# Reordering roundings and subtractions in a two-layer fp32 trunk on one core

## The chip, the cores and the metric

The kernel runs on one core of a Trainium2 chip. The metric is device time in microseconds (us), the median of several runs. TensorE (PE) multiplies; VectorE (DVE) and ScalarE (ACT) work elementwise; GpSimd (POOL) and SyncE (SP) issue loads here. Each engine takes its instructions from a queue of its own, and they meet at semaphores.

## The reference

Two layers, each with a feed-forward block, a mixer and a second feed-forward block, on x of 512 tokens by 1024 channels in float32:

```
x += 0.5 * swiglu_1(rmsnorm(x))
h  = rmsnorm(x);  z = h @ w_in        # pool input, q, k, v, two gate logits
x += (g_pool * P_pool(pool_mixer) + g_attn * P_attn(window_attention)) @ w_out
x += 0.5 * swiglu_2(rmsnorm(x))
swiglu(h): g, u = split(h @ w_gu);  (silu(g) * u) @ w_down      # inner width 2816
```

## The kernel before

**Three products for one.** Every large product is made of three float32r matmuls. Each operand is a pair: a high part (ScalarE rounds the float32 value to float32r by a copy) and a low part (VectorE subtracts the high part from the value, so it must wait for the copy). The terms are high x high, high x low of the weight, low x high of the activation. In the trace `wh` and `wl` are the parts of the weights, `xgh`/`xgl` and `more` those of the activations in the feed-forward block, `op` those in its down product.

**Seven products for eight.** The feed-forward products use a Strassen-like scheme of seven products, in the order `a11, s1, s2, a12, s3, s4, a22`. Its operands are quarters of the activation and combinations of them: B11, T1, T2, B21, T3, B22, T4 in this order for the first product (the gate and up product, a "block"), and in the down product `a11`, f["a"], ... made from the turned results. Combinations of the weights (`sums`) are added on VectorE. A product is run in four segments (c, q), c a half of the contraction with its own weight tile, q a row half; a segment is six matmuls (three in the second half of a 384 column down product). A half product is the two segments of one c. `mid[kind, c, q]` names work that is issued after a segment; `steps[kind]` evacuates the product.

**The inner width** is worked in groups of two blocks and one down product: 384, 512 and 512 columns in ffn0, and 512, 384, 512 in the others. ffn0 and ffn1 are the first and second feed-forward block of layer 0, ffn2 and ffn3 those of layer 1; between ffn0 and ffn1, and between ffn2 and ffn3, stands a mixer. So there are twelve down products, three to a feed-forward block. The last of each is `final`: it also feeds the next norm.

**The norm.** The scale 1/rms is applied after the product, so what is fed is x times the gain. `feed(q, i, pt)` turns a quarter of x (channel pairs q, token half i) with four PE transposes into a PSUM bank, scales it on ScalarE into `xg` (or `more`, when it is kept), and rounds it with `halve`. For a feed-forward block (`halves`) `t1`, `t3`, `t2`, `t4` then combine the kept quarters on VectorE; j counts two tiles of each. T3 has its combination (`t3`) and its rounding (`t3_split`) apart.

**halve and split.** Both round on ScalarE. `split` subtracts at once. `halve` puts the subtraction on the list `unsettled`, and `settle()` issues what stands there:

```
def halve(hi, lo, src):
    nc.scalar.copy(out=hi, in_=src)
    unsettled.append(lambda: nc.vector.tensor_tensor(out=lo, ...))
```

`settle()` runs before each piece of `mid` work and after each product's step, so that a subtraction stands in VectorE's queue behind what was issued meanwhile.

**The order** is written out by hand; the engines keep program order. `W.prep()` after each half product issues, ahead of use, the low part of the weight tile three half products on, the sums, the high part four on, and the loads into seven raw buffers, as they come free (by SP, with the second summand added in by POOL). What a final down product leaves undone for the next block is put on the list `pend` by `left(nxt)`: for a feed-forward block `t3` twice, `t2` twice, two feeds, `t3_split` twice, `t4` twice; for the mixer two feeds. Each call of `due()` takes the next. PSUM holds three tiles of two banks for products (`roles`) and one for turning (`turn`); feeds use a bank of `roles[2]` and one of `turn` by turns.

**The down product** (`down`). The combination `t4` (in the trace `fa<-fa,pt`) reads the turning bank. `high(name, ...)` rounds an operand on ScalarE, `low(name)` subtracts. The updates of x (`x<-mm,x`) stand in the steps of a11, s1, s2, a12, s3, s4, a22; in a final one each quarter of x that is done is squared on ScalarE (`sq`) for the next norm, or stored in the last block.

**The mixer's start.** Two PSUM tiles `late` take the first two pool tiles: `begun(0)` multiplies K tiles 0 to 3 of tile 0, then of tile 1; `begun(1)`, after a part of the q, k, v product, K tiles 4 to 7. K tiles 0 and 1 come from feeds q=0, 2 and 3 from feeds q=1, which are the last feeds of the down product in front.

Of the kernel before, what the change touches and what calls it, by code (L numbers as in the profile page):

```python
# [22 lines left out]
KT = D // P  # L23
# [3 lines left out]
B11, T1, T2, T3, T4, B21, B22 = range(7)  # L27
# [81 lines left out]
def trunk(ctx, tc, x0, xT, consts, vecs, rows, w_g4, w_g3, w_d8, w_d6, w_qkv, w_u, w_pool, w_gate, w_br, w_out, out):  # L109
# [204 lines left out]
    def term(pt, i, n, wh, wl, ah, al):  # L314
        nc.tensor.matmul(pt, wh, ah, start=i == 0, stop=False)
        nc.tensor.matmul(pt, wh, al, start=False, stop=False)
        nc.tensor.matmul(pt, wl, ah, start=False, stop=i == n - 1)
# [30 lines left out]
    class Norm:  # L348
# [61 lines left out]
        def t1(self, j):  # L410
            d = temp("d")
            nc.vector.tensor_tensor(out=d, in0=self.keep[0, j], in1=self.keep[1, j], op=ALU.subtract)
            split(*self.both(T1, j), d)

        def t3(self, j):
            self.keep[4, j] = t = self.place(1, 2, j, F32)
# [2 lines left out]
        def t2(self, j):  # L419
            t = self.keep[0, j]  # L420
            nc.vector.scalar_tensor_tensor(
                out=t, in0=t, scalar=-1.0, in1=self.keep[4, j], op0=ALU.mult, op1=ALU.subtract
            )
            split(*self.both(T2, j), t)

        def t3_split(self, j):
            split(*self.both(T3, j), self.keep[4, j])

        def t4(self, j):
            u = temp("t4")  # L430
            nc.vector.scalar_tensor_tensor(
                out=u, in0=self.keep[0, j], scalar=-1.0, in1=self.keep[3, j], op0=ALU.mult, op1=ALU.subtract
            )
            split(*self.both(T4, j), u)

        def first(self, j, src, scale):
            d = temp("d")[:, :HT]
# [80 lines left out]
    def due(bank=None):  # L518
        if pend:
            pend.pop(0)(bank)  # L520
# [9 lines left out]
    def ffn(ctx, nm, nxt, last):  # L530
# [129 lines left out]
        def low(name):  # L660
            ops.pop((name, "low"))()
# [103 lines left out]
        def down(n, final):  # L765

            jn = n // P

            def add(t, d, c):
                def go(pt):  # L770
                    y = x[:, 2 * t:2 * t + 2, d * S:(d + 1) * S]
                    nc.vector.scalar_tensor_tensor(out=y, in0=pt, scalar=c, in1=y, op0=ALU.mult, op1=ALU.add)
                return go

            def whole(t, d, qs=range(2)):
                if not final:
                    return
                for q in qs:
                    b = 2 * t + q
                    if last:  # L780
                        nc.sync.dma_start(
                            out=out[b * P:(b + 1) * P, d * S:(d + 1) * S], in_=x[:, b, d * S:(d + 1) * S]
                        )
                    else:
                        nxt.squares(d, b)

            def a11(pt):
                add(0, 0, 0.5)(pt)
                return flush

            def s1(pt):
                add(1, 1, -0.5)(pt)
                nc.vector.tensor_tensor(out=f["b"], in0=f["c"], in1=f["b"], op=ALU.subtract)

            def s2(pt):
                add(1, 0, 0.5)(pt)
                low("s3")

            def a12(pt):
                add(0, 0, 0.5)(pt)  # L800
                ops.pop("t4")()
                whole(0, 0)

            def s3(pt):
                add(1, 1, -0.5)(pt)
                low("a22")
                whole(1, 1)

            def s4(pt):
                add(1, 0, 0.5)(pt)  # L810
                whole(1, 0)
                if final:
                    W.sums = None

            def a22(pt):
                y = x[:, 0:2, S:2 * S]
                for q in range(2):
                    nc.vector.scalar_tensor_tensor(
                        out=y[:, q, :], in0=pt[:, q, :], scalar=-0.5, in1=y[:, q, :], op0=ALU.mult, op1=ALU.add
                    )  # L820
                    whole(0, 1, [q])

            mid = {
                ("a11", 1, 0): lambda: low("s2"), ("s1", 0, 1): lambda: low("a12"),
                ("s2", 0, 1): lambda: high("s3", f["b"], n), ("a12", 0, 1): lambda: high("s4", f["c"], n),
                ("s3", 0, 0): lambda: low("s4"), ("s3", 0, 1): lambda: high("a22", f["a"], n),
            }
            if final and nxt is not None:
                spot = [t[:, 0, :] for t in (roles[2], turn)]
                feed = lambda q, t, at: lambda: nxt.feed(q, t, spot[at])  # L830
                mid.update({
                    ("s3", 1, 0): feed(0, 0, 0), ("s3", 1, 1): feed(1, 0, 1), ("s4", 0, 1): feed(2, 1, 0),
                    ("s4", 1, 1): feed(3, 1, 1), ("a22", 0, 1): feed(0, 1, 0), ("a22", 1, 0): feed(1, 1, 1),
                })
                if nxt.halves:
                    mid["a22", 1, 1] = lambda: [nxt.t1(j) for j in range(2)]
                left(nxt)

            strassen(
                ORDER, S, (2, jn - 2), lambda kind, k, q: [ops[kind][:, i, q, k * P:(k + 1) * P] for i in range(2)],  # L840
                dict(a11=a11, s1=s1, s2=s2, a12=a12, s3=s3, s4=s4, a22=a22), mid,
            )

# [5 lines left out]
        for gi, (_, group) in enumerate(groups(nm is first)):  # L849
            for i, n in enumerate(group):  # L850
                if nm is first and gi == i == 0:
                    plain(n, xt, acc, later)
                else:
                    mid = {}
                    if nm is first:
                        if gi == 0:
                            mid["s1", 1, 1] = flush
                    elif gi == i == 0:
                        mid = {at: due for at in (
                            ("a11", 0, 0), ("a11", 0, 1), ("s1", 0, 0), ("s1", 0, 1), ("a12", 0, 0), ("a12", 0, 1),  # L860
                            ("s3", 0, 1), ("s3", 1, 1),
                        )}
                        mid["s1", 1, 1] = lambda: due(turn[:, 0, :])
                        mid["s2", 0, 1] = lambda: due(roles[2][:, 0, :])
                    block(n, i, ORDER, mid)
            down(n, gi == 2)

    @with_exitstack
    def mix(ctx, l, nm, nxt):
# [225 lines left out]
        late = [mm() for _ in range(2)]  # L1095
        w = [W.take("u") for _ in range(2)]

        def begun(h):
            for i in range(2):
                for k, t in enumerate(nm.terms(w[i])[4 * h:4 * h + 4]):  # L1100
                    term(late[i], 4 * h + k, KT, *t)
                if h:
                    W.prep()

        begun(0)
        settle()
        due(side_bank[0])
        for q, width in ((False, 256), (True, 512)):
            pts = [t[:, :width] for t in (mm(), mm(), wide[:, 0, :], wide[:, 1, :])]
            per = CH // width  # L1110
            for c in range(KT // per):
                w_ = W.take("qkv")
                for b in range(NB):
                    for k in range(per):
                        kt, cols = per * c + k, slice(k * width, (k + 1) * width)
                        rows = slice(b % 2 * P, (b % 2 + 1) * P)
                        term(
                            pts[b], kt, KT, *(t[:, kt // 2, b // 2, kt % 2, rows] for t in (nm.h, nm.l)),
                            w_[0][:, cols], w_[1][:, cols],
                        )  # L1120
                    if not q and c == 0 and b == 1:
                        settle()
                        due(side_bank[1])
                    if not q and c == 1 and b == 1:
                        nm.spread(side_bank[1])
                        for i in range(2):
                            pooled(i, late[i])
                if not q and c == 0:
                    settle()
                    nm.sums()  # L1130
                    praw = temp("praw")
                    nc.sync.dma_start(out=praw, in_=w_pool[l])
                    begun(1)
                if c + 1 < KT // per:
                    W.prep()
                if q and c == 1:
                    side(-2)
            for b in range(NB):
                nc.scalar.activation(
                    out=(qs[b] if q else kv[:, b]).rearrange("p h d -> p (h d)"),  # L1140
                    in_=pts[b], func=AF.Copy, scale=nm.rstd[:, b:b + 1],
                )
            W.prep()
            if not q:
                split(*spare[4], praw)
            side(-1 if q else -3)
# [196 lines left out]
```

## Time and profile before

| | |
|---|---|
| median of 3 runs | 1888.84 us (1888.61 to 1888.88) |
| the profiled execution | 1888.9 us, of which the span from the first to the last instruction is 1887.0 us |
| granted TensorE clock | 0.999 |
| busy: PE, VectorE, ScalarE, GpSimd | 98%, 77%, 53%, 7% |
| DMA | 292.80 MB, mean 155 GB/s |

How to read the rows: a row of the timeline is start, length, engine, line, operation, output<-inputs, shape, and in brackets how long the engine stood idle before and who ended that. All instructions have line 97, that of the helper which records them, so rows are told apart by their tiles: `mm`, `sc`, `pt`, `pt_tp`, `pt_pv` are PSUM tiles, `x` is the residual, `cst,x` marks a transpose. A row of the table of waits is engine, output, who ended the wait, us in total, times, longest. A row of the windows is the stretch, its length, and the busy time (count) of PE, weight loads, VectorE, ScalarE and GpSimd, then PE clock, DMA share and GB/s. Starts and lengths are in us.

### The profile page before, as it was taken

The numbers are of one execution on the slowest core, as the hardware profiler recorded it, in microseconds if no ns is written. First come the engines' busy times: TensorE is split into PE (matmuls) and PEld (weight loads), VectorE is DVE, ScalarE is ACT, GpSimd is POOL, SyncE is SP. The second block draws the span as 40 slices with busy tenths as digits, with TensorE's granted clock in tenths as the row PEclk, the third lists the DMA queues.
The fourth block names the chain that finished last, engine by engine and source line by source line (L and its number), as shares of the span: only waits on it lengthen the run. The fifth ranks groups of instructions, "written<-read, shape, count | busy, mean of one in ns | idle before, by whom it ended". The sixth has DMA issues, their size and how long they took to land.

```text
span 1887.0 us, 23912 instructions
## 1 busy us (share of the span) xinstructions
PE 1858.3 (98%) x8928; PEld 1555.4 (82%) x8928; DVE 1448.5 (77%) x1829; ACT 1008.6 (53%) x1493; POOL 124.5 (7%) x152
## 2 busy tenths in 40 slices
PE   9999999999999999999999999999999999999998
PEld 8888888887788788988878898888877887899887
DVE  7878878677564988887988878786675648888878
ACT  6555455645454654555665555555554446545553
POOL 0100000000000001110001001100000000001000
PEclk9999999999999999999999999999999999999999
DMA  8687666322223676777657667753212237667763
GB/s 251 179 229 180 193 174 171 125 80 77 79 89 101 166 199 161 183 204 188 170 158 196 157 179 206 191 166 107 90 68 90 93 86 203 171 168 184 218 179 100
DMA packets 87571, 292.80 MB, mean 155 GB/s; under 512 B 9856, under 2 KB 10112, under 8 KB 87456
## 3 DMA queue, kind: packets, MB, share of 16 engines
q1 hardware_dynamic: 67104, 223.47, 35.1%
q0 software_dynamic: 20208, 67.78, 20.4%
q8 instruction: 70, 1.15, 0.2%
q14 instruction: 45, 0.37, 0.1%
q10 hardware_dynamic: 144, 0.03, 0.0%
HBM read 289.15 MB, written 2.10 MB: 154 GB/s over the span
## 4 chain that ended last, share of the span: by engine, by line
PE 80%; DVE 12%; ACT 6%; issue 1%; DMA 1%; SPq 0%; DVEq 0%; ACTq 0%
PE mm L97 73%; DVE wl L97 4%; PE sc L97 4%; DVE sums L97 2%; PE pt L97 2%; ACT wh L97 2%; PE pt_pv L97 1%; DVE x L97 1%; DVE more L97 1%; ACT xgh L97 1%; DVE op L97 1%; ACT xg L97 1%; PE pt_tp L97 1%; DVE fa L97 1%; ACT sq L97 1%
## 5 line engine op out<-in xcount | busy, mean ns | idle before, releaser
L97 ACT CAST wh<-raw 128x1024 fp32r<-128x1024 f32 (+3 forms) x443 | 432.9, 988 | 274.9 <-PE mm L97 197.0
L97 DVE TENSOR_TENSOR wl<-raw,wh 128x1024 fp32r<-128x1024 f32 (+3 forms) x443 | 502.2, 1146 | 90.5 <-PE mm L97 57.8
L97 PE MATMUL mm<-wh,op 128*128 128x512 f32 x1232 | 392.1, 394 | 2.4 <-DVE op L97 2.4
L97 PE MATMUL mm<-wh,more 128*128 128x512 f32 (+1 forms) x1104 | 335.2, 374 | 3.8 <-ACT more L97 2.6
L97 PE MATMUL mm<-wl,xgh 128*128 128x512 f32 (+2 forms) x840 | 310.4, 370 | 5.9 <-DVE wl L97 5.6
L97 PE MATMUL mm<-wh,xgh 128*128 128x512 f32 (+2 forms) x840 | 312.2, 372 | 1.3 <-ACT xg L97 0.8
L97 PE MATMUL mm<-wh,xgl 128*128 128x512 f32 (+2 forms) x840 | 309.8, 369 | 0.9 <-DVE xgl L97 0.9
L97 PEld LDWEIGHTS mm<-wh,op 128*128 128x128 f32 x1232 | 230.6, 188 | 52.4 <-DVE op L97 5.8
L97 PE MATMUL mm<-wl,op 128*128 128x512 f32 x616 | 240.3, 390 | 1.6 <-DVE wl L97 1.6
L97 PEld LDWEIGHTS mm<-wh,more 128*128 128x128 f32 x1104 | 204.7, 188 | 36.8 <-ACT more L97 3.3
L97 PE MATMUL mm<-wl,more 128*128 128x512 f32 (+1 forms) x552 | 206.6, 374 | 1.7 <-DVE wl L97 1.7
L97 DVE TENSOR_TENSOR wl<-sums,wh 128x1024 fp32r<-128x1024 f32 (+1 forms) x140 | 159.0, 1137 | 45.0 <-ACT wh L97 28.7
L97 ACT CAST wh<-sums 128x1024 fp32r<-128x1024 f32 (+1 forms) x140 | 136.2, 981 | 95.0 <-DVE sums L97 52.2
L97 PEld LDWEIGHTS mm<-wl,xgh 128*128 128x128 f32 x840 | 157.9, 188 | 31.1 <-DVE wl L97 10.3
L97 PEld LDWEIGHTS mm<-wh,xgh 128*128 128x128 f32 x840 | 157.8, 188 | 23.5 <-ACT xg L97 2.1
L97 PEld LDWEIGHTS mm<-wh,xgl 128*128 128x128 f32 x840 | 157.8, 188 | 23.2 <-DVE xgl L97 2.1
L97 POOL DMA_DIRECT2D raw<-in_w_g x92 | 79.5, 864 | 1325.5 <-DMA raw<-in_w_g 591.6
L97 PEld LDWEIGHTS mm<-wl,op 128*128 128x128 f32 x616 | 115.8, 188 | 26.2 <-DVE wl L97 3.3
L97 PE MATMUL mm<-xgh,wh 128*128 128x512 f32 x320 | 129.4, 404 | 0.4 <-ACT xgh L97 0.4
L97 PE MATMUL mm<-xgl,wh 128*128 128x512 f32 x320 | 125.3, 392 | 0.4 <-DVE xgl L97 0.4
L97 PE MATMUL mm<-xgh,wl 128*128 128x512 f32 x320 | 125.2, 391 | 0.0
L97 PEld LDWEIGHTS mm<-wl,more 128*128 128x128 f32 x552 | 103.6, 188 | 18.5 <-DVE wl L97 3.3
(247 smaller groups left out, 2397.7 us busy)
## 6 DMA issues: line engine op xcount, KB each, us to landing
raw<-in_w_g SPq DMA_DIRECT2D x160, 512.0 KB, 5.0
raw<-in_w_d SPq DMA_DIRECT2D x100, 512.0 KB, 4.5
raw<-in_w_g POOLq DMA_DIRECT2D x64, 512.0 KB, 6.9
raw<-in_w_g SPq DMA_DIRECT2D x77, 384.0 KB, 4.3
raw<-in_w_d POOLq DMA_DIRECT2D x40, 512.0 KB, 5.5
raw<-in_w_gate SPq DMA_DIRECT2D x32, 512.0 KB, 3.2
raw<-in_w_g POOLq DMA_DIRECT2D x28, 384.0 KB, 5.8
raw<-in_w_br SPq DMA_DIRECT2D x16, 512.0 KB, 3.2
```

What stands on the lines that cost most here:

```text
L97: return lambda *args, **kw: self.tc.keep_in_program_order(call(*args, **kw))
```

## The change

Five edits.

1. `t1`, `t2`, `t3_split` and `t4` of the norm use `halve` instead of `split`: the rounding is issued at once, the subtraction at the next `settle()`.
2. In every down product `t4` moves from the step of a12 to behind the first segment of s3, and the low part of s4 from there into the step of a12; the high part of a22 moves from the second to the third segment of s3, its low part from the step of s3 to behind the first segment of s4.
3. In final down products that feed a norm, the first feed moves from the third to the second segment of s3, and the third feed from the second to the third segment of s4.
4. In the first block after a mixer or down product (not in ffn0) the first `t2` comes behind the third segment of a11 and the second behind the first of s1 (they were behind the first and second of s1), and the two feeds behind the third segment of s1 and the first of s2 (they were behind the fourth of s1 and the second of s2).
5. The mixer's first two tiles take K tiles 0 and 1 of both tiles, then 2 and 3 of both.

```diff
@@ Norm
         def t1(self, j):
-            split(*self.both(T1, j), d)
+            halve(*self.both(T1, j), d)
...
-            split(*self.both(T2, j), t)
+            halve(*self.both(T2, j), t)
...
-            split(*self.both(T3, j), self.keep[4, j])
+            halve(*self.both(T3, j), self.keep[4, j])
...
-            split(*self.both(T4, j), u)
+            halve(*self.both(T4, j), u)
@@ down
             def a12(pt):
                 add(0, 0, 0.5)(pt)
-                ops.pop("t4")()
+                low("s4")
                 whole(0, 0)
             def s3(pt):
                 add(1, 1, -0.5)(pt)
-                low("a22")
                 whole(1, 1)
...
-                ("s3", 0, 0): lambda: low("s4"), ("s3", 0, 1): lambda: high("a22", f["a"], n),
+                ("s3", 0, 0): lambda: ops.pop("t4")(), ("s3", 1, 0): lambda: high("a22", f["a"], n),
+                ("s4", 0, 0): lambda: low("a22"),
...
-                    ("s3", 1, 0): feed(0, 0, 0), ("s3", 1, 1): feed(1, 0, 1), ("s4", 0, 1): feed(2, 1, 0),
+                    ("s3", 0, 1): feed(0, 0, 0), ("s3", 1, 1): feed(1, 0, 1), ("s4", 1, 0): feed(2, 1, 0),
@@ ffn
-                            ("a11", 0, 0), ("a11", 0, 1), ("s1", 0, 0), ("s1", 0, 1), ("a12", 0, 0), ("a12", 0, 1),
+                            ("a11", 0, 0), ("a11", 0, 1), ("a11", 1, 0), ("s1", 0, 0), ("a12", 0, 0), ("a12", 0, 1),
                             ("s3", 0, 1), ("s3", 1, 1),
...
-                        mid["s1", 1, 1] = lambda: due(turn[:, 0, :])
-                        mid["s2", 0, 1] = lambda: due(roles[2][:, 0, :])
+                        mid["s1", 1, 0] = lambda: due(turn[:, 0, :])
+                        mid["s2", 0, 0] = lambda: due(roles[2][:, 0, :])
@@ mix
-        def begun(h):
+        def begun(ks):
             for i in range(2):
-                for k, t in enumerate(nm.terms(w[i])[4 * h:4 * h + 4]):
-                    term(late[i], 4 * h + k, KT, *t)
-                if h:
+                terms = nm.terms(w[i])
+                for k in ks:
+                    term(late[i], k, KT, *terms[k])
+                if ks[-1] == KT - 1:
                     W.prep()
-        begun(0)
+        begun((0, 1))
+        begun((2, 3))
...
-                    begun(1)
+                    begun((4, 5, 6, 7))
```

## Prediction

> **What bounds the kernel now.** I read the page's busy times first, then the table of waits, then two stretches by windows, then the timeline around each stretch the diff touches.
>
> ```profile
> PE 1858.3 (98%) x8928; PEld 1555.4 (82%) x8928; DVE 1448.5 (77%) x1829; ACT 1008.6 (53%) x1493; POOL 124.5 (7%) x152
> PE mm L97 <- DVE op L97: 2.4, 9, 0.4
> 606.00:656.00 50.00, 46.75 (x206) 36.13 (x205) 41.66 (x58) 33.40 (x48) 3.45 (x4) 1.00 0.51 137
> 656.00:690.00 34.00, 34.00 (x155) 28.24 (x154) 25.79 (x24) 17.51 (x21) 2.59 (x3) 1.00 0.77 215
> ```
>
> PE is the bound nearly everywhere: 34.00 us busy of the 34.00 from 656 on. So only PE's waits can be won. The change alters no instruction's size and no engine's count, only the order on VectorE, ScalarE and PE. From 606 to 656 (ffn1's first block) PE idles 3.25 us and VectorE works 41.66 of 50.
>
> Idle time understates a wait, because a matmul's bar overlaps the next. These rows of an ordinary 512 column down show it:
>
> ```profile
> 213.56 0.62 PE L97 MATMUL mm<-wh,op 128*128 128x512 f32 x2
> 214.01 0.39 PE L97 MATMUL mm<-wl,op 128*128 128x512 f32 x1
> 214.59 0.73 PE L97 MATMUL mm<-wh,op 128*128 128x512 f32 x2 [0.19 <-DVE op L97]
> 622.14 0.50 PE L97 MATMUL mm<-wh,more 128*128 128x512 f32 x1 [0.70 <-ACT more L97]
> 622.48 0.40 PE L97 MATMUL mm<-wl,more 128*128 128x512 f32 x1
> ```
>
> Two matmuls start in 214.01 - 213.56 = 0.45, so one start takes 0.227. The next start comes after 0.58: 0.35 lost, where the bar tells of 0.19. After a wait the following start also takes longer (622.14 to 622.48, 0.34): 0.11 more. So I price waits from starts: 0.35 + 0.11 = 0.46 here. [...]
>
> **The downs.** There are 12: five of 512 columns without feeds, four of 384, three final ones with feeds.
>
> ```profile
> 209.92 1.22 DVE L97 SCALAR_TENSOR_TENSOR x<-mm,x 128x1024 f32<-128x1024 f32 x1
> 211.06 1.21 DVE L97 SCALAR_TENSOR_TENSOR fa<-fa,pt 128x1024 f32<-128x1024 f32 x1
> 212.18 1.22 DVE L97 TENSOR_TENSOR wl<-sums,wh 128x1024 fp32r<-128x1024 f32 x1
> 213.32 1.22 DVE L97 TENSOR_TENSOR op<-fc,op 128x1024 fp32r<-128x1024 f32 x1
> 816.57 0.50 PE L97 MATMUL mm<-wl,op 128*128 128x512 f32 x1 [0.42 <-DVE wl L97]
> 817.44 0.73 PE L97 MATMUL mm<-wh,op 128*128 128x512 f32 x2 [0.37 <-DVE op L97]
> 819.04 0.95 DVE L97 TENSOR_TENSOR op<-fa,op 128x768 fp32r<-128x768 f32 x1
> ```
>
> VectorE runs x, t4 (`fa`), weight low, then s4's own low; 1024 columns take 1.135 from start to start. The change swaps t4 and s4's low: the low then ends at 212.3, before PE asks at 214.24, and the weight low stays where it was. Gain 0.46. t4 ends at 214.5, a22's high copy at 215.6, a22's low third behind the x update at 219.1; its product starts at 219.2 and reads it at 219.7. Covered. Five times 0.46 = 2.3.
>
> In a 384 down s4 waits twice: for the weight low (816.57), unchanged, then for the low: 817.44 - 816.57 - 0.227 = 0.64, which goes. But a22's low (819.04) now runs behind the weight low of its product: they change places, so it starts at 819.04 + 1.135 and ends at 821.12. PE, 0.64 early, asks at 821.0: a new wait of 0.17 + 0.11. Gain 0.36, four times 1.4. With no restart cost it is 1.9; with a full VectorE instruction more in front (1.135) a loss of 3.1.
>
> **Final downs into the mixer (ffn0, ffn2).**
>
> ```profile
> 337.14 0.52 PE L97 MATMUL mm<-cst,x 128*128 128x128 f32 x3 [1.07 <-ACT xgh L97]
> 341.57 1.22 DVE L97 SCALAR_TENSOR_TENSOR x<-mm,x 128x1024 f32<-128x1024 f32 x1
> 342.99 0.63 ACT L97 ACTIVATE sq<-x 128x512 f32<-128x512 f32 x1
> 346.68 0.69 DVE L97 TENSOR_TENSOR xgl<-xg,xgh 128x512 fp32r<-128x512 f32 x1 [0.17 <-ACT xgh L97]
> 347.47 0.46 PE L97 MATMUL mm<-xgl,wh 128*128 128x512 f32 x1
> 349.03 0.51 PE L97 MATMUL mm<-xgh,wh 128*128 128x512 f32 x1 [0.18 <-ACT xgh L97]
> 349.76 0.50 PE L97 MATMUL mm<-xgl,wh 128*128 128x512 f32 x1 [0.22 <-DVE xgl L97]
> 353.74 0.27 PE L97 MATMUL pt_tp<-cst,x 128*128 128x128 f32 x1
> ```
>
> The feed at 337.14 waits 1.2 for s3's x update (1.07 idle and 0.39 - 0.227 of the last bar). One segment later (six matmuls, 1.36) it need not wait. But PE does not keep the 1.2. t4, now one instruction pair later, ends at 333.0 and holds the turning bank for the second feed (0.3 lost); s4's x update stands behind lows of the feeds, at 341.7, so the feed in a22 waits 0.6 for it; and ScalarE's squares of it start at 343.0 as before, so the mixer's first low is ready at 347.37 as before. PE's second mixer matmul starts at 347.42 instead of 347.47: 0.05 won, bounds 0 and 0.6.
>
> There the new K order pays. Second K pair starts before: 349.03 and 349.76; from 347.47 to the transpose at 353.74 are 6.27 for 23 starts, 5.22 without waits. Twelve matmuls of both tiles' first K pair now come first, so PE asks for the second pair at 350.0, after the lows (349.7). Gain 6.27 - 5.22 - 0.11 = 0.94. Together 1.0, twice 2.0.
>
> **First blocks (ffn1, ffn3).** Here T1 to T4 are rounded and subtracted.
>
> ```profile
>   ACT more L97: 3.2, 4
> 616.14 1.22 DVE L97 TENSOR_TENSOR wl<-raw,wh 128x1024 fp32r<-128x1024 f32 x1
> 620.75 0.69 DVE L97 SCALAR_TENSOR_TENSOR more<-more 128x512 f32<-128x512 f32 x1
> 622.12 0.69 DVE L97 TENSOR_TENSOR more<-more 128x512 fp32r<-128x512 f32 x1 [0.69 <-ACT more L97]
> 626.44 0.69 DVE L97 TENSOR_TENSOR xgl<-xg,xgh 128x512 fp32r<-128x512 f32 x1 [0.51 <-ACT xgh L97]
> 634.98 1.29 DVE L97 TENSOR_TENSOR more<-more 128x512 fp32r<-128x512 f32 x2
> 638.45 1.22 DVE L97 TENSOR_TENSOR r<-r,mm 128x1024 f32<-128x1024 f32 x1
> 642.53 0.69 DVE L97 TENSOR_TENSOR more<-t,more 128x512 fp32r<-128x512 f32 x1 [1.13 <-ACT more L97]
> 615.70 1.00 ACT L97 COPY r<-mm 128x1024 f32<-128x1024 f32 x1
> 640.81 0.39 PE L97 MATMUL mm<-wh,xgh 128*128 128x512 f32 x1
> 644.41 0.50 PE L97 MATMUL mm<-wl,xgh 128*128 128x512 f32 x1 [0.49 <-DVE wl L97]
> 647.62 0.47 PE L97 MATMUL mm<-wh,more 128*128 128x512 f32 x1 [0.41 <-ACT wh L97]
> 648.66 0.50 PE L97 MATMUL mm<-wl,more 128*128 128x512 f32 x1 [0.57 <-DVE wl L97]
> 654.01 1.03 PE L97 MATMUL pt<-cst,p 128*128 128x128 f32 x8
> ```
>
> The first row is from the view of the `more` tiles in this block: VectorE sat idle 3.2 us, in front of four subtractions, until ScalarE had rounded. I walked the three queues instruction by instruction with these durations (on VectorE 1.135 and 0.605 from start to start); in the old order the walk meets every row above within 0.1. In the new order:
> - VectorE: T2's first combination directly behind the weight low of 616.14, at 617.3 instead of 620.75; two sums 617.9 and 619.0; weight low 620.5; T2's first low 621.65; second combination 622.3; weight low 622.9; second low 624.0. The first rounding stands on ScalarE ahead of r's copy (now 618.5, was 615.70) and of s2's weight highs (0.9 later). s2 still starts at 621.1, 1.0 earlier; it then waits 0.6 for the weight low and T2's low, and half the gain stays.
> - T2's two stalls go, but the B21 low then waits for ScalarE (T2's rounding, a weight high, two scalings, its own rounding: 623.0 to 626.0) until 626.0, was 626.44. VectorE is 0.44 ahead, and so up to T3's first low (634.5).
> - T3's second low is settled only after r's add. Behind the first one stand a weight low (635.1), a sum (636.3) and r (637.4, was 638.45); it starts at 638.55 instead of 635.6. PE asks at 638.1 and waits until 639.28. So s4 starts at 641.65, 0.84 later than 640.81. This is the price of the deferral.
> - T4's two stalls go, so the weight lows of s4 and a22 come in time. The waits of 644.41, 647.62 and 648.66 (0.65, 0.58, 0.82, and 0.11 twice) go: 2.3.
> - The block ends at 652.53 instead of 654.01: 1.5 won, twice 3.0.
>
> [...] If VectorE could pass r's add, T3's waits would go and the time would be 1873.8.
>
> **Final down into ffn2.**
>
> ```profile
> 948.31 0.69 DVE L97 TENSOR_TENSOR xgl<-d,xgh 128x512 fp32r<-128x512 f32 x1 [1.09 <-ACT xgh L97]
> 992.40 1.03 PE L97 MATMUL pt<-cst,p 128*128 128x128 f32 x8
> ```
>
> T1 is made here on a full VectorE, and its stalls (1.09 at the first) delay s1's weight low. Settled behind x's last update, the two subtractions find their rounding done, and the weight low comes 1.26 earlier. The same walk, with PE 0.66 early from the down, meets the same T3 wait (1.2) and ends the block at 989.5: 2.9 won.
>
> **Sum.** 2.3 + 1.4 + 2.0 + 3.0 + 2.9 = 11.6. The profiled execution took 1888.9 (span 1887.0), 0.06 over the median 1888.84. Forecast 1888.9 - 11.5 = 1877.4, rounding the small wins down. Left at zero: SyncE's and POOL's queues (loads are issued by the same calls, and raw buffers come free no later), PE's instruction count, and the five temporaries alive at once between T1's rounding and subtraction in the mixer's tail (six buffers; with a seventh one copy would wait about 0.7).
>
> **Rivals.**
> - T3's low is not late, because VectorE is further ahead than 0.44: three waits of 1.2 less, 1873.8. For it: 1.4 us of idle VectorE in front of the B21 low in my walk. Against: three 1.135 instructions stand before it.
> - The first blocks give nothing, as VectorE's 41.66 of 50 is the true limit and each removed stall returns in front of another ScalarE result. Then only 2.3 + 1.4 + 2.0 remain: 1883.2. For it: the B21 low does just that. Against: the waits after 644 follow VectorE stalls directly.
> - Slower: deferred lows arrive behind PE. Six lows of T2, T3, T4 per block; the forecast has one late by 1.2. With the other five late too: 15 x 1.2 = 18.0, 1895.4. It decides from 3.8 us more per block. Against: T2's and T4's lows have 0.6 us or less of wait in the walk.
> - The swap does nothing: each wait returns one product later, as the 384 downs show in part; 1888.9.
>
> **Chances.** Forecast 0.60 (own range 1875.0 to 1880.5), T3 in time 0.12, first blocks nothing 0.17, nothing at all 0.06, slower 0.05. About 0.2%, 3.8 us, is what a measurement tells from no change: faster 0.89, same 0.06, slower 0.05. The range 1873.6 to 1882.6 holds the first two and half of the third.
>
> **What would show it.** In the trace after: no wait of PE on `op` at s4 in the 512 downs, one at a22 in the 384 ones; no wait over 0.3 in the mixer's first 24 matmuls; VectorE idle before `more` subtractions under 1 us per block; a PE wait of about 1.2 at the third matmul of s3's second half, and none at s4 and a22. The prediction is wrong if that wait exceeds 3 us, or if new PE waits on `x` or the turning bank appear in final downs beyond 0.6.

## The result, and the profile after

The changed kernel takes 1876.01 us (median of 4 runs, 1875.56 to 1876.13). The kernel before took 1888.72 us beside it (4 runs, 1888.13 to 1888.88). The ratio is 0.9933, with a 95% interval of 0.9916 to 0.9950: 12.7 us faster. The forecast was 1877.4. The profiled execution took 1876.13 us with a span of 1874.3 us, against 1887.0 before, at a granted clock of 1.000.

From the page, the table of waits and the windows of the changed kernel; the window is ffn1's first block, shifted by the 2.22 us that are won up to there:

```profile
PE 1853.7 (99%) x8928; PEld 1556.5 (83%) x8928; DVE 1447.0 (77%) x1829; ACT 1009.1 (54%) x1493; POOL 124.1 (7%) x152
PE mm L97 <- DVE wl L97: 6.6, 12, 1.1
PE mm L97 <- DVE more L97: 3.0, 3, 1.0
PE mm L97 <- DVE x L97: 0.7, 3, 0.2
DVE more L97 <- ACT more L97: 13.7, 8, 2.6
603.78:653.78 50.00, 47.54 (x214) 37.59 (x213) 44.06 (x61) 33.52 (x48) 3.45 (x4) 1.00 0.53 143
```

The same numbers of instructions run on every engine. The row of nine waits on `op` is gone, and three new waits on `more` stand in its place, one to each of the first blocks of ffn1, ffn2 and ffn3. VectorE fits 61 instructions into the 50 us instead of 58. For comparison, from the waits of the kernel before:

```profile
DVE more L97 <- ACT more L97: 23.3, 20, 2.6
```

Twelve stalls of VectorE that waited for ScalarE's rounding, 9.6 us, are gone: all that stood in the three first blocks. The eight that are left lie in the mixers.

To place the gain I compare starts of the same matmul in both traces, at the edges of each place. "Won" is by how much the far edge came earlier than the near one did, in us:

| place | forecast | won |
|---|---|---|
| five 512 downs | 5 x 0.46 | 0.51, 0.49, 0.53, 0.53, 0.53 |
| four 384 downs | 4 x 0.36 | 0.35, 0.30, 0.34, 0.37 |
| end of ffn0, ffn2 and mixer's start | 2 x 1.0 | 0.92, 1.02 |
| first block of ffn1, ffn3 | 2 x 1.5 | 1.67, 1.79 |
| final down of ffn1 and first block of ffn2 | 2.9 | 2.99 |
| sum | 11.6 | 12.34 |

The remaining 0.3 lies in stretches that the change doesn't touch: the first 50 us, which differ from trace to trace (last section), came 0.18 earlier.

**Downs.** VectorE and PE in a 512 down, then in a 384 down, from the timeline:

```profile
210.44 1.22 DVE L97 TENSOR_TENSOR op<-fc,op 128x1024 fp32r<-128x1024 f32 x1
211.57 1.22 DVE L97 TENSOR_TENSOR wl<-sums,wh 128x1024 fp32r<-128x1024 f32 x1
212.71 1.22 DVE L97 SCALAR_TENSOR_TENSOR fa<-fa,pt 128x1024 f32<-128x1024 f32 x1
213.40 0.39 PE L97 MATMUL mm<-wl,op 128*128 128x512 f32 x1
213.63 0.62 PE L97 MATMUL mm<-wh,op 128*128 128x512 f32 x2
...
815.78 0.95 DVE L97 TENSOR_TENSOR op<-fa,op 128x768 fp32r<-128x768 f32 x1
816.40 0.39 PE L97 MATMUL mm<-wl,op 128*128 128x512 f32 x1
816.79 0.74 PE L97 MATMUL mm<-wh,op 128*128 128x512 f32 x2
817.37 0.40 PE L97 MATMUL mm<-wl,op 128*128 128x512 f32 x1
```

In the 512 down the low of s4 (`op<-fc,op`) now runs first, and PE starts at its pace of 0.23 with no wait. In the 384 down the new wait is where it was forecast: a22's low ends at 816.73, and PE starts at 816.79, 0.39 behind the start before instead of 0.227, so 0.16 late (forecast 0.17).

**First block of ffn1**, VectorE and PE:

```profile
617.92 0.69 DVE L97 TENSOR_TENSOR more<-more 128x512 fp32r<-128x512 f32 x1
618.53 1.22 DVE L97 TENSOR_TENSOR wl<-sums,wh 128x1024 fp32r<-128x1024 f32 x1
623.37 0.69 DVE L97 TENSOR_TENSOR xgl<-xg,xgh 128x512 fp32r<-128x512 f32 x1 [1.28 <-ACT xgh L97]
634.93 1.21 DVE L97 TENSOR_TENSOR r<-r,mm 128x1024 f32<-128x1024 f32 x1
636.06 0.69 DVE L97 TENSOR_TENSOR more<-more 128x512 fp32r<-128x512 f32 x1
642.57 2.35 DVE L97 TENSOR_TENSOR wl<-raw,wh 128x1024 fp32r<-128x1024 f32 x2
619.80 0.50 PE L97 MATMUL mm<-wl,more 128*128 128x512 f32 x1 [0.34 <-DVE wl L97]
625.99 0.50 PE L97 MATMUL mm<-wh,xgh 128*128 128x512 f32 x1 [0.21 <-ACT xg L97]
629.92 0.50 PE L97 MATMUL mm<-wh,xgl 128*128 128x512 f32 x1 [0.46 <-DVE xgl L97]
636.80 0.74 PE L97 MATMUL mm<-wh,more 128*128 128x512 f32 x2 [0.98 <-DVE more L97]
639.24 0.39 PE L97 MATMUL mm<-wh,xgh 128*128 128x512 f32 x1
650.12 1.03 PE L97 MATMUL pt<-cst,p 128*128 128x128 f32 x8
```

T3's second low (636.06) stands behind r's add (634.93), and PE waits for it at 636.80. s4 starts at 639.24. No wait is left in s4 and a22, and the transposes that follow the block start at 650.12. Three smaller waits stand ahead of that: s2's weight low (619.80), a12's bank (625.99) and B21's second low (629.92), for which PE idled 0.32 before (632.85).

### The profile page after: what moved, and what is told of

It reads as the page before. It is cut to its first block, busy times and chain, and to the rows that moved or that the text cites. A ratio compares the mean times of both kernels' runs of the same rounds, so it can differ in the third digit from the quotient of the medians.

```text
span 1874.3 us, 23908 instructions
## 1 busy us (share of the span) xinstructions
PE 1853.7 (99%) x8928; PEld 1556.5 (83%) x8928; DVE 1447.0 (77%) x1829; ACT 1009.1 (54%) x1493; POOL 124.1 (7%) x152
## 4 chain that ended last, share of the span: by engine, by line
PE 84%; DVE 9%; ACT 4%; issue 1%; DMA 1%; SPq 0%; DVEq 0%; ACTq 0%
PE mm L97 77%; PE sc L97 4%; DVE wl L97 3%; PE pt L97 2%; DVE sums L97 1%; ACT wh L97 1%; PE pt_pv L97 1%; DVE x L97 1%; DVE more L97 1%; PE pt_tp L97 1%; ACT xgh L97 1%; ACT xg L97 1%; ACT sq L97 1%; DVE xgl L97 0%; DVE op L97 0%
```

## The experiments

Each was timed beside the kernel before (1888.67 to 1888.82 us in those comparisons).

**1. The downs that feed no norm, alone.** The new order in the nine of them, the old one in the three final ones:

```diff
+            fed = final and nxt is not None
...
-                ops.pop("t4")()
+                if fed:
+                    ops.pop("t4")()
+                else:
+                    low("s4")
 ... (the other moves of edit 2 in the same way)
```

> Of the change only the new order of t4, s4's low part and a22's parts, in the nine down products that feed no norm. Theory A, each place wins what its own PE waits cost and the places add up: five 512 column downs 0.52 each and four 384 column downs 0.34 each (the steps between the traces before and after), 3.9 us less than before, about 1884.8. Rival B, a wait removed in a down comes back in the next block, where VectorE is busy as well: less than 2 us, 1887 or more.

Measured 1885.04 us, ratio 0.9979 (0.9971 to 0.9988). In the trace the 512 downs win 0.49 to 0.53 each and the 384 ones 0.33 to 0.37, and no later block gives any of it back. Priced by their idle time (2.4 in the table of waits before), these waits were worth less than the 3.8 that the time shows; the starts priced them rightly (2.3 + 1.4 = 3.7).

**2. The mixer's K order, alone** (edit 5):

```diff
-        begun(0)
+        begun((0, 1))
+        begun((2, 3))
```

> Of the change only the K order of the mixer's first two tiles. Theory A: the second K pair is asked for after its low part is ready (350.0 against 349.7 in the walk), so the waits 0.35, 0.50 and 0.11 go in both mixers: 1.9 us less than before, 1886.8. Rival B, the mixer starts when ScalarE's last feeds are done, whatever PE does first: the wait moves to the transposes behind the 24 matmuls, nothing gained, 1888.7.

Measured 1887.27 us, ratio 0.9991 (0.9982 to 1.0000). The time alone hardly tells it from no change (1.55 us, and the first 50 us of this trace took 0.8 longer than in the kernel before); the trace does: from the mixer's first matmul to the transposes behind the 24 matmuls 0.96 and 0.98 are won, at the two mixers, and the two waits at the second K pair are gone.

**3. The three final downs put back** in the changed kernel (edit 3 undone, and edit 2 in those three), and **4. the new order in all twelve downs** in the kernel before (edits 2 and 3 alone). The lines of 3:

```diff
-                    ("s3", 0, 1): feed(0, 0, 0), ("s3", 1, 1): feed(1, 0, 1), ("s4", 1, 0): feed(2, 1, 0),
+                    ("s3", 1, 0): feed(0, 0, 0), ("s3", 1, 1): feed(1, 0, 1), ("s4", 0, 1): feed(2, 1, 0),
 ... (edit 2 undone where the down feeds a norm)
```

> The changed kernel with the order of the three final down products that feed a norm as it was before (edit 3 undone, and edit 2 in these three). Theory A (the earlier feeds only move where PE waits: the two mixers' starts are bounded by the norm's results, ffn2's first block by VectorE): about the same, 1876.0 to 1876.4. Theory B (PE keeps the time that it saves at the feeds, 0.45 to 0.55 at each of the three places): 1876.0 + 1.5 = 1877.5. Theory C (the mixer gains its second 0.45 only if the feeds come sooner): 1876.0 + 0.9 = 1876.9.

> The kernel before with the new order of the down products, the three final ones with their earlier feeds among them; the norm's combinations, the first blocks' places and the mixer's K order are as before. Theory A (the earlier feeds save PE 1.2 each at one place, but the second feed's bank, the x update and ScalarE's squares take it back by the mixer's first low, and the first block of ffn2, bound by VectorE, absorbs its start of 0.55): no more than the nine other downs gave alone, 1885.04 - 0.1 to 0.3 = about 1884.8. Theory B (what is saved at the feeds is kept): 1885.04 - 3 x 0.9 = about 1882.3.

Measured 1876.34 us (1875.51 to 1876.64; the changed kernel 1876.01) and 1884.77 us (the nine downs alone 1885.04). So the earlier feeds and the final downs' order are worth 0.3 at most, which the spread of the runs doesn't tell from nothing. The timeline shows why. First the changed kernel, with the feed in a22, the mixer's first low and the transposes that follow the 24 matmuls:

```profile
341.83 0.63 PE L97 MATMUL mm<-cst,x 128*128 128x128 f32 x4 [0.23 <-DVE x L97]
345.51 0.41 PE L97 MATMUL mm<-xgh,wh 128*128 128x512 f32 x1
346.16 0.51 PE L97 MATMUL mm<-xgl,wh 128*128 128x512 f32 x1 [0.23 <-DVE xgl L97]
351.56 0.60 PE L97 MATMUL pt_tp<-cst,x 128*128 128x128 f32 x4
```

Then the kernel with the final downs put back:

```profile
335.43 0.63 PE L97 MATMUL mm<-cst,x 128*128 128x128 f32 x4 [1.08 <-ACT xgh L97]
345.53 0.39 PE L97 MATMUL mm<-xgh,wh 128*128 128x512 f32 x1
345.75 0.45 PE L97 MATMUL mm<-xgl,wh 128*128 128x512 f32 x1
351.08 0.60 PE L97 MATMUL pt_tp<-cst,x 128*128 128x128 f32 x4
953.71 0.50 PE L97 MATMUL mm<-wl,more 128*128 128x512 f32 x1
```

And the kernel with the new order in all downs but the old K order:

```profile
346.08 0.50 PE L97 MATMUL mm<-xgl,wh 128*128 128x512 f32 x1 [0.23 <-DVE xgl L97]
347.69 0.49 PE L97 MATMUL mm<-xgh,wh 128*128 128x512 f32 x1 [0.18 <-ACT xgh L97]
348.42 0.50 PE L97 MATMUL mm<-xgl,wh 128*128 128x512 f32 x1 [0.23 <-DVE xgl L97]
```

With the old feeds PE waits 1.08 idle at the third one, and finds the mixer's first low ready. With the new ones it doesn't wait there, but at the feed in a22 and again for that low (0.42 between the starts beyond its pace). In the trace with the old final downs the kernel's start came 0.47 earlier than in that of the changed kernel, so 0.47 is added to its rows before they are compared: with the new feeds PE is 0.49 earlier at the mixer's first matmul (345.51 against 346.00) and no earlier at the transposes (351.56 against 351.55). Only the K order wins at this place. In ffn2 it is the same: PE enters the block 0.55 earlier, and loses 0.48 of it at s2's weight low (954.33 in the changed kernel, below), where it is 0.54 behind its pace; with the old final downs it is 0.06 behind (953.71, above).

```profile
954.33 0.50 PE L97 MATMUL mm<-wl,more 128*128 128x512 f32 x1 [0.38 <-DVE wl L97]
```

**5. The norm's combinations, alone**: `halve` for `split` in all four, and the places of edit 4, in the kernel before.

> Of the change only the later subtractions of T1 to T4 and the earlier t2 and feeds in the first blocks. Theory A: ffn1 1.7, ffn3 1.8, and ffn2 2.9, because ffn2's block ends by VectorE's queue and not by when PE enters it: 6.4 us less than before, 1882.3. Rival B, ffn2's block needs the earlier entry that the moved feeds give (0.55): 5.8 us less, 1882.9, and a first a12 product of ffn2 that is later by 0.5. The trace decides between them.

Measured 1882.08 us, ratio 0.9964 (0.9950 to 0.9977). The three first blocks win 1.82, 3.10 and 1.86: 6.78 by the trace, 6.74 by the time. ffn2 wins all of its 2.99 without the 0.55 of the down in front, as in experiment 3.

**6. T4's subtraction put off, alone; 7. T3's, alone,** both in the kernel before:

```diff
 def t4(self, j):
-            split(*self.both(T4, j), u)
+            halve(*self.both(T4, j), u)
 def t3_split(self, j):               # 7, instead
-            split(*self.both(T3, j), self.keep[4, j])
+            halve(*self.both(T3, j), self.keep[4, j])
```

> The kernel before with T4's subtraction alone put off. Theory A (T4's two stalls on VectorE are what makes the weight lows of s4 and a22 late): each of the three first blocks ends 1.3 earlier, 1888.8 - 3.9 = 1884.9. Theory B (the end of the block is set by VectorE's whole load, and a stall that is removed at T4 comes back at the next result of ScalarE): no block wins over 0.3, 1888.0 or more.

> The kernel before with T3's subtraction alone put off; all else as before. Theory A (the delay behind r's add is a wait of about 1.2 us for PE in s3's second half, but VectorE's two idle gaps in front of T3's subtractions also go, so the weight lows after it come as early or earlier and the block wins a little in the end): the wait stands in the trace, and each of the three first blocks (ffn1, ffn2, ffn3) ends about 0.46 earlier: 1888.8 - 1.4 = 1887.4. Theory B (as the prediction priced it, 1.2 lost where it stands and never taken back): 1888.8 + 3.6 = 1892.4.

T4 alone: 1884.88 us, ratio 0.9979 (0.9971 to 0.9988), 1.26, 1.24 and 1.28 won in the blocks. Of the three waits of PE in s4 and a22 one is left:

```profile
647.10 0.50 PE L97 MATMUL mm<-wl,more 128*128 128x512 f32 x1 [0.68 <-DVE wl L97]
```

T3 alone: 1887.44 us, ratio 0.9994 (0.9985 to 1.0002). The interval holds no change, but it excludes 1892.4, and each of the three blocks ends 0.38 to 0.45 earlier in the trace. Its timeline:

```profile
639.25 0.68 DVE L97 TENSOR_TENSOR more<-more 128x512 fp32r<-128x512 f32 x1
642.36 0.69 DVE L97 TENSOR_TENSOR more<-t,more 128x512 fp32r<-128x512 f32 x1 [0.69 <-ACT more L97]
639.99 0.73 PE L97 MATMUL mm<-wh,more 128*128 128x512 f32 x2 [0.98 <-DVE more L97]
648.49 0.50 PE L97 MATMUL mm<-wl,more 128*128 128x512 f32 x1 [0.27 <-DVE wl L97]
```

The wait that the prediction called the price stands there in full, and the block ends earlier all the same. PE loses 1.26 at it, and its waits in s4 and a22 are 1.7 shorter: it was going to wait there anyhow, and the block wins the 0.45 by which they shrink further. Theory A has the right sum, but names the wrong stall. The kernel before has no stall in front of T3's subtractions (634.98 runs as one row of two); what shrinks is VectorE's first stall at T4, 0.69 (642.36) instead of 1.13 (642.53 before), since r's add no longer stands behind T3's second low and so r's add (638.12, before at 638.45), the silu and T4's rounding come sooner.

**8. T3 subtracted at once** in the changed kernel, all else as changed:

```diff
 def t3_split(self, j):
-            halve(*self.both(T3, j), self.keep[4, j])
+            split(*self.both(T3, j), self.keep[4, j])
```

> The changed kernel, but T3 rounded and subtracted at once as before. In the prediction the wait of 1.2 us per block at the second half of s3 was the price of the deferral. Theory A, that price is absorbed: without the wait PE reaches the end of the block 1.2 earlier and there waits for p, which VectorE finishes 0.6 later as r's add stands behind T3's second low; 0.3 to 0.45 per block is won, total 1874.9. Rival B, the wait is lost time as the prediction priced it: 1.2 per block and more, 3.5 us less than the changed kernel, 1872.5.

Measured 1875.40 us (1874.96 to 1875.55), ratio to before 0.9928 (0.9915 to 0.9940). The wait at T3 is gone, and another one is there: not for p at the block's end, where theory A put it, but at a22's weight low. VectorE and PE of this kernel:

```profile
638.95 1.23 DVE L97 TENSOR_TENSOR wl<-sums,wh 128x1024 fp32r<-128x1024 f32 x1 [0.62 <-ACT wh L97]
643.03 2.36 DVE L97 TENSOR_TENSOR wl<-raw,wh 128x1024 fp32r<-128x1024 f32 x2
644.30 0.50 PE L97 MATMUL mm<-wl,more 128*128 128x512 f32 x1 [0.69 <-DVE wl L97]
```

Of 1.26 that T3's wait cost PE, 0.3 to 0.5 per block is won in the trace (1.2 in all; the medians differ by 0.6). The rest is waited for at a22's weight low, which VectorE starts at 643.03 here and at 642.57 in the changed kernel.

**9. T2 and the two feeds at their old places** in the changed kernel (edit 4 undone):

```diff
-                            ("a11", 0, 0), ("a11", 0, 1), ("a11", 1, 0), ("s1", 0, 0), ("a12", 0, 0), ("a12", 0, 1),
+                            ("a11", 0, 0), ("a11", 0, 1), ("s1", 0, 0), ("s1", 0, 1), ("a12", 0, 0), ("a12", 0, 1),
 ... (the feeds of s1 and s2 one segment later)
```

> The changed kernel with the first blocks' T2 and their two feeds at the old places (edit 4 undone). Theory A (T2 moved directly behind the weight low of a11 is what brings s2's weight low and the B21 low forward): each of the three first blocks ends about 0.9 later, 1876.0 + 2.6 = 1878.6. Theory B (the subtraction put off is all that matters, the place of T2 nothing): 1876.0, and VectorE idles no more in front of the subtractions than in the changed kernel.

Measured 1878.22 us, ratio 0.9944 (0.9932 to 0.9957): 2.2 later than the changed kernel; the blocks win 0.71, 0.71 and 0.80 less (0.9 was expected). VectorE again stalls for the first rounding, and PE at s2:

```profile
619.62 0.69 DVE L97 TENSOR_TENSOR more<-more 128x512 fp32r<-128x512 f32 x1 [0.68 <-ACT more L97]
619.64 0.50 PE L97 MATMUL mm<-wh,more 128*128 128x512 f32 x1 [0.69 <-ACT more L97]
```

**10 and 11. Versions built on this.** Number 8 shows that VectorE's next stall is for ScalarE's rounding of a weight (0.62 at 638.95), which stands behind the silu of r. In 10 the silu of the first block is issued behind that rounding, with T3 at once. In 11 the silu is moved in the same way, T3's subtractions stay put off as in the changed kernel, and the second is settled ahead of r's add:

```diff
 def block(n, i, order, mid):
     count[0] += 1
+    first = count[0] == 1
 ...
 def a12(pt):
+                settle()                  # 11 only
                 nc.vector.tensor_tensor(out=r, in0=r, in1=pt, op=ALU.add)
-                for q in range(2):
-                    nc.scalar.activation(out=r[:, q, :], in_=r[:, q, :], func=AF.Silu, scale=rs(q))
+                def gate():
+                    for q in range(2):
+                        nc.scalar.activation(out=r[:, q, :], in_=r[:, q, :], func=AF.Silu, scale=rs(q))
+
+                if first:                 # the first block of each feed-forward
+                    return gate
+                gate()
```

> The kernel with T3 subtracted at once, and in the first block of each feed-forward the silu of r issued on ScalarE behind the next weight tile's rounding, not ahead of it. Theory A (what is left of the block is VectorE's queue, where the 0.62 idle in front of s4's second weight low, which waits for ScalarE's rounding behind the silu, is passed on to a22's weight low, where PE waits 0.85): the block ends about 0.46 earlier, 1875.4 - 1.4 = 1874.0. Theory B (a22's weight low is late for want of VectorE time alone, so the idle comes back in front of T4's subtraction): 1875.4.

> The changed kernel with T3's second subtraction settled ahead of r's add instead of behind it, and in the first block the silu of r issued on ScalarE behind the next weight tile's rounding. Theory A (the subtraction is then just in time for PE at s3's second half, with no stall of VectorE at T3 and none in front of s4's second weight low): each of the three first blocks ends 0.7 earlier than with T3 at once, 1875.4 - 2.1 = 1873.3. Theory B (what is gained is taken by p's last product on VectorE at the block's end): as T3 at once, 1875.4.

Number 10 measured 1874.08 us, ratio 0.9922 (0.9908 to 0.9935). Number 11 measured 1873.34 us (1872.55 to 1873.62), ratio 0.9918 (0.9905 to 0.9932), and beats the changed kernel's 1876.01: its slowest run is 1.9 us under the other's fastest, with the kernel before within 0.05 in both comparisons. First rows of VectorE, PE and ScalarE from 10:

```profile
640.57 0.69 DVE L97 TENSOR_TENSOR more<-t,more 128x512 fp32r<-128x512 f32 x1 [0.33 <-ACT more L97]
644.78 0.50 PE L97 MATMUL mm<-wl,more 128*128 128x512 f32 x1 [0.40 <-DVE wl L97]
637.39 1.28 ACT L97 ACT_TABLE_LOAD   x1
638.69 1.34 ACT L97 ACTIVATE r<-r,rstd 128x512 f32<-128x512 f32 x2
```

Then of VectorE and PE from 11:

```profile
635.48 0.69 DVE L97 TENSOR_TENSOR more<-more 128x512 fp32r<-128x512 f32 x1
636.22 0.74 PE L97 MATMUL mm<-wh,more 128*128 128x512 f32 x2
644.32 0.47 PE L97 MATMUL mm<-wl,more 128*128 128x512 f32 x1
```

In 10 half of the stall comes back at T4 (0.33), and PE still waits at a22. By the rows this stall comes from an `ACT_TABLE_LOAD` of 1.28 us in front of the silu (637.39, 638.69), and T4's rounding stands behind both. In the kernel before this load runs while ScalarE waits for r's add (636.22, the silu at 639.70); here it runs when the silu could. No run tests this apart. In 11 T3's low is ready as PE asks (636.22, no idle), VectorE has no stall from T3 to T4, and PE passes a22's weight low with no idle. Against the kernel before its first blocks win 2.83, 3.61 and 2.84, where the changed kernel wins 1.67, 2.44 and 1.79 (ffn2 without the 0.55 of its down). Number 11 changes two things at once, and no run has the earlier settling alone, so its share is not shown.

## Why the prediction was right, point by point

- **Downs: right, a little small.** The swap, the cover of t4 and a22's high copy, and the new wait at a22 of the 384 downs are all where they were put. The term of the 512 downs was 0.46 and measured 0.49 to 0.53. The prediction let one start after a wait be late (by 0.11); in the trace before, the five to ten starts behind that one take up to 0.240 instead of 0.227, and these sum to the missing 0.03 to 0.07. The term of the 384 downs was 0.36 and measured 0.30 to 0.37.
- **Final downs into the mixer: right in sum and in its two parts.** Priced: 0.05 from the feeds, 0.94 from the K order. Measured: 0.3 at most for all three final downs, and 0.96 to 0.98. The new waits on the turning bank and on x were priced at 0.3 and 0.6; by their starts they cost 0.2 and 0.4, and the first feed, now a segment earlier, waits another 0.17 for x (328.39; the update ends at 328.34), which had no price. The low that stops the mixer's second matmul was forecast to let it start at 347.42; it starts at 346.16, which is 347.41 with the 1.25 that were won ahead of this place. So one sign is met by idle time only: no idle over 0.3 stands in the first 24 matmuls (0.23), but from start to start that wait costs 0.42.
- **First blocks: right in the waits that it names, 1.5 against 1.67 and 1.79.** The term that is off is how far VectorE gets ahead: 0.44 at the B21 low by the walk, but 623.37 is 0.85 earlier than 626.44 once the 2.22 of the entry are taken off. The walk put T2's first low behind s2's weight low; it runs ahead of it (617.92, then 618.53), in time in which the weight low would still have waited for its rounding (on ScalarE two of them take 2.00 from 617.20). Of the 0.41 that this is beyond the walk, 0.26 is left where PE starts behind T3's low, and 0.19 at the block's end. VectorE has no stall left in front of `more` subtractions here (under 1 us was forecast). Edit 4 is worth 2.2 of the time, by experiment 9.
- **The wait at T3: right in place and size, wrong as a price.** 1.2 was forecast, and from start to start it costs 1.145 and 0.115 for the restart. But "if T3's low were in time, 1873.8" took three times 1.2 as the gain. With T3 at once the time is 1875.40, since PE then waits at a22. The wait was costed where it stands; its cost is only what is not waited for later in the same block. The prediction's sum wasn't hurt, because its walk went on to the block's end; the rival's was. Of these runs only experiment 11, which also moves the silu, gets down to that rival's time.
- **Final down into ffn2: 2.9 against 2.99, and its cause narrower than said.** All of it comes from edits 1 and 4 (3.10 alone); of the 0.55 from the down in front (0.66 was forecast) 0.48 is lost at s2. T1's stalls are gone and s1's weight low comes earlier, as the prediction said: less the 4.69 that were won ahead of this down, the low behind T1's subtractions (946.11) is 1.30 earlier than before (952.10), and 1.26 was forecast. The rows, of VectorE and then of PE at the block's end:

```profile
944.91 1.29 DVE L97 TENSOR_TENSOR xgl<-d,xgh 128x512 fp32r<-128x512 f32 x2
984.72 1.03 PE L97 MATMUL pt<-cst,p 128*128 128x128 f32 x8
```

- **The other rivals.** "The first blocks give nothing" falls with experiments 5 and 6, "the swap does nothing" with experiment 1, and "slower" with the table of waits: of the lows of T2, T3 and T4 only T3's second makes PE wait, once in each block. Nor does VectorE pass r's add: in the changed kernel both of T3's roundings end on ScalarE at 630.48, and the second low starts at 636.06, behind the add (634.93). In the kernel before, VectorE idles 0.69 in front of T2's first subtraction (622.12), though T2's second combination (622.73), which needs no rounding, stands right behind it.

By parts, from the times: nine downs 3.8, K order 1.6 (1.9 by the starts), norm 6.7, final downs 0.3 or nothing, together 12.4 of the 12.7. The parts add up because they meet in different places. Inside a block they don't: by the medians T3's deferral wins 1.3 alone and costs 0.6 beside the other edits.

## What to carry to other kernels

A wait that was removed was worth only what the same engine didn't wait for later in the same stage (T3's cost PE 1.26, and 0.3 to 0.5 per block was won without it): walk the queues on to the end of the stage before pricing it. A rounding on one engine and its subtraction on another needed only to be issued apart, with other work between them: here twelve stalls of VectorE, 9.6 us, are gone with edits 1 and 4. Issue the subtraction ahead of the first instruction that isn't needed sooner, and then look for what the other engine has put in front of the next rounding. Ask of an operation that you move what else moves with it, such as the `ACT_TABLE_LOAD` of 1.28 us in front of the silu. And an earlier start of a stage that another engine bounds may be worth nothing: here the 0.49 and 0.55 that the final downs won were given back almost whole.

## What was not expected of the hardware

How well three queues can be followed by hand. The walks that gave the expectations of 6, 7 and 11 used fixed durations for each kind of instruction, and the times came out at 1884.88 for 1884.9, 1887.44 for 1887.4 and 1873.34 for 1873.3. That they agree to 0.1 is partly luck: experiments 2, 8 and 9 missed by 0.4 to 0.5, and the walks don't hold the start of the kernel. The same matmul of ffn0 starts at 50.11 us in the trace before, and at 50.63, 50.93 and 49.85 in experiments 1, 2 and 4, which change nothing ahead of it. Why is open. So the traces are compared by the steps at the places, not by their spans.
